# A two-layer decoder step on one core: a fifth raw weight tile in the place of a state tile, the samples' gathers moved to GpSimd, and score banks copied out twice instead of three times

## The chip, the cores and the metric

The kernel runs on one core of one Trainium2 chip. The metric is device microseconds (us) from the start to the end of one execution of the program. The engines that matter are the tensor engine (PE in the profile; PEld is its weight load), the vector engine (DVE), the scalar engine (ACT), GpSimd (POOL) and the sync engine (SP), whose queue issues nearly all DMAs here.

## What is computed

One inference step of a two-layer trunk: 272 prompt positions (16 learned ones and 256 given ones) and 8 samples of one position each share all weights, so that every product has 280 columns. Layer 0 is RWKV-7 time mixing with 64 heads of 64; layer 1 is sliding-window attention over one shared K and V. The change touches layer 0 alone:

```python
def rwkv7_step(S, inp):
    r, d, k, v, kk, b = inp
    sa = jnp.einsum('bhij,bhj->bhi', S, kk)
    S = S * d[:, :, None, :] - sa[..., None] * b[:, :, None, :] + v[..., None] * k[:, :, None, :]
    return S, jnp.einsum('bhij,bhj->bhi', S, r)

def rwkv7_layer(xn, shift_prev, S0, ...):
    rkvz = jnp.einsum('btpd,pde->btpe', xm[:, :, :4], w_rkvz)      # 4 products, 2048 x 4096 each
    ...                                                            # r, k, v, z, decay d, kk, b per head
    S_fin, y = lax.scan(rwkv7_step, S0, (r, d, k, v, kk, b))       # prompt: 272 steps; samples: 1 step each
    ...                                                            # group norm of y, bonus, gate silu(z)
    return y @ w_out, S_fin, xn[:, -1]
```

## The kernel before

**Products.** All weights come from memory as float32 tiles of 128 x 512 (256 KB, two blocks of 128 rows by 256 columns), named `raw_...` (line 200). ACT casts each to a high part `whi` (line 184), DVE subtracts to get the low part `wlo` (line 186), and PE multiplies three times per block: `whi` by the high and by the low part of the activations and `wlo` by the high part (lines 207 to 209). `raw` has four buffers, `whi` and `wlo` five each. In the stages after layer 0's middle part a second pool `rawx` of four takes every other tile.

**The long middle part** (`phase_a`, in the profile some 150 to 1350 us) runs these products and, between them, the recurrence of the prompt as matrix algebra on chunks of 64 positions. `drive` (line 590) writes the order of PE by hand. It counts positions, one per piece of a product (`products`, line 689: six matmuls of 128 x 128 by 280). Side streams are generators: what they yield is the number of positions until they are taken up again, or a condition. `main` (644) runs the chains of chunks (`chain`), the scores and the solving of triangular blocks; `preps` (662) prepares two heads' pairs at a time (`prep`, u = 0 to 15); `decodes` (681) does the samples; `late_gates` (1376) loads the gated activations for the output product once the last chain and the last group of samples are done. All other engines get an order from a scheduler that follows PE's positions and their dependences; each engine then works through its own queue in order, and so does SP.

**prep** (836) loads `kT`, `rT` and `vT` by DMA, computes `kk`, `a` (its tile is named `ta`) and the decay products `Pp`, and gathers the eight samples' columns of six tensors in one tile `sm`: six copies of 128 x 16 on ACT (line 910). PE transposes `sm` eight positions after `vT` was asked for (913).

**scores** (960) multiplies keys with queries in PSUM banks `ps_sc` (992) and empties each bank with ACT copies to `ND` (997, 998) and `N12` (999), beside two masked multiplications on DVE (1000, 1002). `substitute` (1033) takes `ND` on POOL (lines 1044 to 1047: `Noff`, `nd`, `N16`), then DVE inverts blocks of 16 in place and transposes them (`NL`, `TN`). `solve` (1069) waits a fixed number of positions and joins the blocks on PE (`ps_so`, 1082 to 1109) with copies by DVE and ACT between them (`ET`, `TT`, 1104 and 1112); `N12` is read at 1100.

**decode** (1246) goes through the samples' states, 16 heads at a time (g = 0 to 3), in eight slices of 256 KB: DMA to `dS` (1271), then two multiplications to `dT` and two sums on DVE (1275, 1276). `dS` has two buffers, and slices advance only while `self.samples` is true, that is while a chain runs. A slice is asked for right after the one before it was used, and used 8 positions later (5 for g = 3).

## Time and profile before

| | us |
|---|---|
| median of 3 runs | 2190.12 |
| lowest and highest of them | 2186.92, 2193.9 |
| the profiled execution, its own time | 2201.98 |
| span of its instructions | 2200.2 |

The profiled execution is 0.5% above the median. The profile names idle time of an engine with what ended it ("<- ACT cl L861" is a wait that ended when ACT had written `cl` at line 861). Numbers of buffers and layers in names are left out, so that `ps_so` stands for all banks of the solving. In the views of waits the three numbers are the us in total, the times, and the longest one. In the timeline a bracket gives the idle time before an instruction and what ended it. In the windows an engine's number is its busy time and the bracket the count of its instructions; PEclk is the share of TensorE's clock that was granted. A busy PE is not PE at its peak, since the ends of its matmuls are modelled.

### The profile page before, as it was taken

How to read it: one execution, taken by the hardware profiler on the slowest of the kernel's cores; microseconds unless marked ns; L12 is line 12 of the kernel's file. 1: busy time of each engine (PE TensorE's matmuls, PEld its weight loads, DVE VectorE, ACT ScalarE, POOL GpSimd, SP SyncE). 2: the span in 40 equal slices, each digit the busy share in tenths (PEclk: the TensorE clock that was granted, in tenths of full speed). 3: DMA queues.
4: the chain of work that ended last, by engine and by line, in shares of the span. 5: the costliest groups of instructions: out<-in, count | busy, mean ns of one | idle time of the engine just before them, and what ended most of it. 6: DMA issues, size and time to landing. Idle time of an engine off the chain costs nothing.

```text
span 2200.2 us, 56108 instructions
## 1 busy us (share of the span) xinstructions
PE 2122.6 (96%) x21556; PEld 2015.7 (92%) x21556; DVE 1716.4 (78%) x4115; ACT 1272.9 (58%) x2916; POOL 83.4 (4%) x100
## 2 busy tenths in 40 slices
PE   9999999999999998999999999999999999999997
PEld 7998899999889898888889899998999999999997
DVE  7956767787587776877887786997888888888885
ACT  3456756675666656756666454564565556555443
POOL 0010000000000000100001000110000000000000
PEclk9999999999999999999999999999999999999999
DMA  6997667757656776665645878766554544577774
GB/s 235 320 316 233 191 192 236 210 175 258 198 171 187 235 226 178 203 196 173 207 138 156 276 228 251 241 213 200 157 160 139 168 145 135 167 209 242 231 225 136
DMA packets 277444, 448.51 MB, mean 204 GB/s; under 512 B 53352, under 2 KB 99112, under 8 KB 276784
## 3 DMA queue, kind: packets, MB, share of 16 engines
q1 hardware_dynamic: 276888, 443.89, 65.1%
q8 instruction: 169, 2.77, 0.5%
q10 hardware_dynamic: 288, 1.05, 0.1%
q14 instruction: 99, 0.81, 0.1%
HBM read 382.81 MB, written 66.15 MB: 204 GB/s over the span
## 4 chain that ended last, share of the span: by engine, by line
PE 82%; DMA 6%; DVE 6%; ACT 4%; issue 2%; SPq 0%; DVEq 0%; POOLq 0%; ACTq 0%
PE ps_z L207 6%; PE ps_z L208 5%; PE ps_z L209 5%; PE ps_ob L209 3%; PE ps_ob L208 3%; PE ps_v L207 3%; PE ps_ob L207 3%; PE ps_q L209 3%; PE ps_q L207 3%; PE ps_q L208 3%; PE ps_k L207 3%; PE ps_v L208 3%; PE ps_v L209 3%; PE ps_k L209 2%; PE ps_k L208 2%; PE ps_r L207 2%
## 5 line engine op out<-in xcount | busy, mean ns | idle before, releaser
L207 PE MATMUL ps_z<-mhlm,whi_z 128*128 128x280 f32 x512 | 160.9, 314 | 1.1 <-ACT st L770 1.1
L208 PE MATMUL ps_z<-mhlm,whi_z 128*128 128x280 f32 x512 | 152.2, 297 | 2.1 <-issue 2.1
L207 PE MATMUL ps_q<-bmh,whi_qb 128*128 128x264 f32 x512 | 150.5, 294 | 2.4 <-ACT whi_qb L184 2.4
L209 PE MATMUL ps_z<-mhlm,wlo_z 128*128 128x280 f32 x512 | 152.0, 297 | 0.0
L209 PE MATMUL ps_q<-bmh,wlo_qb 128*128 128x264 f32 x512 | 146.7, 286 | 1.5 <-DVE wlo_qb L186 1.5
L207 PE MATMUL ps_z<-bmh,whi_zb 128*128 128x264 f32 x512 | 147.5, 288 | 0.0
L208 PE MATMUL ps_q<-bml,whi_qb 128*128 128x264 f32 x512 | 146.1, 285 | 0.0
L208 PE MATMUL ps_z<-bml,whi_zb 128*128 128x264 f32 x512 | 145.5, 284 | 0.0
L209 PE MATMUL ps_z<-bmh,wlo_zb 128*128 128x264 f32 x512 | 145.5, 284 | 0.0
L207 PE MATMUL ps_ob<-ghi,whi_ob 128*128 128x264 f32 x512 | 145.3, 285 | 0.0
L209 PE MATMUL ps_ob<-ghi,wlo_ob 128*128 128x264 f32 x512 | 144.9, 285 | 0.0
L208 PE MATMUL ps_ob<-glo,whi_ob 128*128 128x264 f32 x512 | 144.5, 283 | 0.0
L186 DVE TENSOR_TENSOR wlo_r<-raw_r,whi_r 128x512 fp32r<-128x512 f32 x128 | 87.8, 688 | 64.9 <-ACT whi_r L184 63.9
L184 ACT CAST whi_oa<-raw_oa 128x512 fp32r<-128x512 f32 x128 | 78.9, 620 | 101.2 <-DMA raw_oa<-a_w_out 31.7
L184 ACT CAST whi_ob<-raw_ob 128x512 fp32r<-128x512 f32 x128 | 79.2, 621 | 97.1 <-PE ps_ob L208 80.2
L186 DVE TENSOR_TENSOR wlo_v<-raw_v,whi_v 128x512 fp32r<-128x512 f32 x128 | 87.9, 691 | 53.0 <-ACT whi_v L184 48.7
L207 PE MATMUL ps_k<-mhlm,whi_k 128*128 128x280 f32 x384 | 121.9, 317 | 1.9 <-ACT whi_k L184 1.6
L207 PE MATMUL ps_v<-mhlm,whi_v 128*128 128x280 f32 x384 | 121.4, 316 | 1.9 <-ACT st L770 1.9
L186 DVE TENSOR_TENSOR wlo_z<-raw_z,whi_z 128x512 fp32r<-128x512 f32 x128 | 88.6, 695 | 35.7 <-ACT whi_z L184 32.7
L186 DVE TENSOR_TENSOR wlo_oa<-raw_oa,whi_oa 128x512 fp32r<-128x512 f32 x128 | 87.5, 689 | 35.4 <-ACT whi_oa L184 31.7
L186 DVE TENSOR_TENSOR wlo_k<-raw_k,whi_k 128x512 fp32r<-128x512 f32 x112 | 76.0, 687 | 49.5 <-ACT whi_k L184 49.1
L184 ACT CAST whi_zb<-raw_zb 128x512 fp32r<-128x512 f32 x128 | 78.3, 619 | 62.5 <-PE ps_z L208 42.0
(462 smaller groups left out, 7739.5 us busy)
## 6 DMA issues: line engine op xcount, KB each, us to landing
raw_k<-a_w_rkvz SPq DMA_DIRECT2D x128, 256.0 KB
raw_v<-a_w_rkvz SPq DMA_DIRECT2D x128, 256.0 KB
raw_r<-a_w_rkvz SPq DMA_DIRECT2D x128, 256.0 KB
raw_z<-a_w_rkvz SPq DMA_DIRECT2D x128, 256.0 KB
raw_oa<-a_w_out SPq DMA_DIRECT2D x128, 256.0 KB
raw_qb<-b_w_qz SPq DMA_DIRECT2D x128, 256.0 KB
raw_zb<-b_w_qz SPq DMA_DIRECT2D x128, 256.0 KB
raw_ob<-b_w_o SPq DMA_DIRECT2D x128, 256.0 KB
```

The costliest lines, as they stand in the source:

```text
L184: self.nc.scalar.copy(hi, src)
L186: return self.nc.vector.tensor_tensor(lo, src, hi.bitcast(F32), op=ALU.subtract)
L207: mm(ps, wh, xh, start=start, stop=False)
L208: mm(ps, wh, xl, start=False, stop=False)
L209: return mm(ps, wl, xh, start=False, stop=stop)
```

## The change

Four edits:

- `raw` gets five buffers instead of four, `dS` one instead of two. A slice of the samples' state is now asked for 3 positions after the one before it was used, and used 5 positions later (4 for g = 3).
- The six gathering copies of `prep` go from ACT to POOL (16 preps, so 96 copies).
- `ND` and `N12` become two halves of one tile `F`. For the upper 32 rows of a half bank one ACT copy of 64 columns takes the place of two of 32: 64 copies fewer. `F` is one tile for the whole kernel, where `N12` was taken anew for each chain.
- By the yields the streams stand at other positions.

```diff
             else:
-                raw = t("raw", F32, bufs=4)
+                raw = t("raw", F32, bufs=5)
...
-        self.ND = t([128, 20, 32], "ND")
+        self.F = t([128, 20, 64], "F")
+        self.ND, self.N12 = self.F[:, :, 0:32], self.F[:, 0:16, 32:64]
...
         for i, x in enumerate((kk, a, kT, rT, vT, Pp[:, :, 5:])):
-            A.copy(sm[:, :, i], x[:, :, L:N])
+            G.tensor_copy(sm[:, :, i], x[:, :, L:N])
...
-        if u % 2 == 0:
-            self.N12 = rp.tile([128, 16, 32], F32, tag="N12", name=f"N12_{u}")
-        N12 = self.N12
...
-                A.copy(inst(self.ND, r1, cs), pv[r1, :, :, 0:32])
+                A.copy(inst(self.F, r1, cs), pv[r1, :, :, 0:64])
                 A.copy(inst(self.ND, r2, cs), pv[r2, :, :, 32:64])
-                A.copy(inst(N12, r1, cs), pv[r1, :, :, 32:64])
...
         for q in range(64 // NI):
-            S = rp.tile([128, NI, 64], F32, tag="dS", bufs=2, name=f"dS{g}_{q}")
+            if q:
+                yield 3
+            S = rp.tile([128, NI, 64], F32, tag="dS", bufs=1, name=f"dS{g}_{q}")
             T = rp.tile([128, NI, 64], F32, tag="dT", bufs=1, name=f"dT{g}_{q}")
             ...
-            yield 8 if g < 3 else 5, lambda: self.samples
+            yield 5 if g < 3 else 4, lambda: self.samples
```

The first place where the order differs is POOL's queue at the fourth substitution (the tile `sm` belongs to the prep of u = 8, the four other rows to the substitution). Before:

```order
L1047 TENSOR_TENSOR Noff<-ND,consts 128x16x16
L1044 TENSOR_TENSOR nd_9508<-ND,consts 128x320
L1045 TENSOR_TENSOR nd_9509<-ND,consts 128x320
L1046 TENSOR_TENSOR N_1734<-nd_9508,nd_9509 128x320
L1133 MEMSET X_4_11387 64x256 x2
```

After:

```order
L911 COPY sm_10058<-rT_9632 128x2x8
L1044 TENSOR_TENSOR Noff<-F,consts 128x16x16
L911 COPY sm_10058<-kk_9634 128x2x8
L911 COPY sm_10058<-Pp 128x2x8
L1041 TENSOR_TENSOR nd_9546<-F,consts 128x320
L1042 TENSOR_TENSOR nd_9547<-F,consts 128x320
L1043 TENSOR_TENSOR N_1734<-nd_9546,nd_9547 128x320
```

Three gathers now stand ahead of `nd` in POOL's queue.

The second place is SP's queue at the last group of samples (`dS3`), between the raw tiles of the first output product. Before:

```order
L1271 DMA dS3_3_19278<-state_wkv 128x1x512
L200 DMA raw_oa1_512_6_19397<-a_w_out 128x512
L200 DMA raw_oa1_512_8_19466<-a_w_out 128x512
L1271 DMA dS3_4_19363<-state_wkv 128x1x512
L200 DMA raw_oa1_512_10_19507<-a_w_out 128x512
L200 DMA raw_oa1_512_12_19545<-a_w_out 128x512
L1271 DMA dS3_5_19457<-state_wkv 128x1x512
```

After:

```order
L1270 DMA dS3_4_19558<-state_wkv 128x1x512
L781 DMA xd_159<-xr1_4_19223 128x2x280
L200 DMA raw_oa1_1024_2_19719<-a_w_out 128x512
L718 DMA xr1_8_19759<-xT 128x2x280
L200 DMA raw_oa1_1024_4_19761<-a_w_out 128x512
L1270 DMA dS3_5_19669<-state_wkv 128x1x512
```

The slices stand two product groups later (column 1024 instead of 512), and the transposition `ps_dy` of the last group stands 27 positions later on PE, while the last chain (`ps_wu` of chain 7) stands 13 positions later; the end of the first output product stays where it was.

The third place is SP's queue where `late_gates` loads `gy` and `gz` (560 or 544 KB each). Before:

```order
L1360 DMA gy4_20068<-yd4_216 128x1120
L1360 DMA gy5_20105<-yd5_217 128x1120
L200 DMA raw_oa1_1280_0_20118<-a_w_out 128x512
L200 DMA raw_oa1_1280_2_20149<-a_w_out 128x512
L1358 DMA gz6_20137<-zd6_194 128x1120
L717 DMA xr1_10_20172<-xT 128x2x280
L200 DMA raw_oa1_1280_4_20174<-a_w_out 128x512
L1358 DMA gz7_20344<-zd7_195 128x1120
```

After:

```order
L1359 DMA gy4_20261<-yd4_216 128x1120
L1359 DMA gy5_20298<-yd5_217 128x1120
L1357 DMA gz6_20341<-zd6_194 128x1120
L1357 DMA gz7_20396<-zd7_195 128x1120
L200 DMA raw_oa1_1536_14_20365<-a_w_out 128x512
```

The four loads stand later, and no raw tile stands between them.

More of the change, by code (lines that the diff above doesn't have):

```diff
@@ L573, in phase_a @@
         ms = nc.gpsimd.memset
-        for a in (self.KB, self.ND, self.N16, self.Noff, self.Y):
+        for a in (self.KB, self.F, self.N16, self.Noff, self.Y):
             ms(a, 0.0)
```

## The prediction

> **What bounds the kernel now.** I read the page first, then busy time by stretches, then who PE and ACT wait for, then the timeline at the waits.

> ```profile
> PE 2122.6 (96%) x21556; PEld 2015.7 (92%) x21556; DVE 1716.4 (78%) x4115; ACT 1272.9 (58%) x2916; POOL 83.4 (4%) x100
> PE 82%; DMA 6%; DVE 6%; ACT 4%; issue 2%; SPq 0%; DVEq 0%; POOLq 0%; ACTq 0%
> 1350.00:1400.00 50.00, 50.00 (x389) 50.00 (x388) 38.17 (x62) 24.33 (x44) 5.42 (x6) 1.00 0.74 224
> 150.00:1300.00 1150.00, 1096.83 (x13429) 1024.11 (x13428) 875.35 (x1948) 735.50 (x1745) 45.10 (x47) 0.98 0.66 202
> 1300.00:1500.00 200.00, 194.94 (x1488) 191.95 (x1487) 167.79 (x311) 104.00 (x187) 16.84 (x18) 1.00 0.77 238
> 1500.00:1900.00 400.00, 396.17 (x3361) 381.13 (x3360) 323.83 (x1188) 228.53 (x620) 1.10 (x2) 1.00 0.51 157
> ```

> PE is the bound: 2122.6 of 2200.2 us, and 82% of the chain. No edit takes work from PE, so the change can only win PE's idle time and clock. In the stretch 150 to 1300, where three of the edits act, PE is idle for 1150 - 1096.83 = 53.2 us, and it was granted 0.98 of its clock, which is some 23 us more. From 1300 to 1900 only 5.1 + 3.8 us are idle. A change that won all of it would stop at some 80 us; what can be won is that part of it which ends on ACT or on a raw tile.

> ```profile
> PE ps_l L207 <- ACT cl L861: 5.5, 6, 2.0
> PE ps_so L1109 <- ACT ET L1104: 4.6, 3, 1.9
> PE ps_q L207 <- ACT whi_qb L184: 2.4, 1, 2.4
> PE ps_k L207 <- ACT whi_k L184: 1.6, 1, 1.6
> PE ps_sm L913 <- ACT sm L910: 1.6, 2, 1.2
> ACT sm L910 <- DMA rT<-rd: 24.7, 15, 4.2
> ACT sm L910 <- DMA vT<-vd: 15.2, 8, 4.3
> ACT whi_k L184 <- DMA raw_k<-a_w_rkvz: 22.0, 12, 7.1
> ACT whi_r L184 <- DMA raw_r<-a_w_rkvz: 20.8, 12, 3.6
> ```

> PE's waits are small and scattered, and ACT ends most of the ones above. ACT itself stands 24.7 + 15.2 = 39.9 us at the gathering copies, waiting for a tile of which it wants eight columns. Everything queued behind on ACT stands with it.

> **The gathers leave ACT.** Two places show what such a wait costs PE:

> ```profile
> 828.76 0.20 ACT L910 COPY sm<-rT 128x16 f32<-128x16 f32 x1 [4.25 <-DMA rT<-rd]
> 829.29 0.74 ACT L1183 COPY X<-ps_wu 64x256 f32<-64x256 f32 x2
> 829.70 1.07 PE L1184 MATMUL ps_sy<-X,BK 128*64 128x64 f32 x16 [1.60 <-ACT X L1183]
> 966.81 0.21 ACT L910 COPY sm<-rT 128x16 f32<-128x16 f32 x1 [2.17 <-DMA rT<-rd]
> 967.04 0.58 ACT L1104 COPY ET<-ps_so 32x512 f32<-32x512 f32 x1
> 967.67 1.82 PE L1109 MATMUL ps_so<-TT,ET 32*32 32x32 f32 x64 [1.91 <-ACT ET L1104]
> 829.50:835.00 5.50, 5.24 (x48) 4.97 (x49) 4.04 (x9) 2.21 (x6) 0.00 (x0) 0.69 1.03 296
> 967.50:975.00 7.50, 7.33 (x106) 7.00 (x108) 3.22 (x6) 3.80 (x10) 0.00 (x0) 0.54 0.60 160
> ```

> ACT stood 4.25 us for `rT`, the copy of `X` came late, and PE stood 1.60 us; the second time it was 1.91 us behind `ET`. Right after both, PE ran on a reduced clock: (1 - 0.69) x 5.5 = 1.7 us and (1 - 0.54) x 7.5 = 3.45 us of work lost. With the 1.6 us in which PE waited for `sm` itself this is 1.60 + 1.91 + 5.15 + 1.6 = 10.3 us. POOL, busy for 4% of the span, waits instead, and PE reads `sm` only eight positions after `vT` was asked for. Bounds: 5.2 us if the clock drops anyway and POOL brings `sm` no sooner (1.60 + 1.91 + 1.7); 13 if one more clock drop goes (another 3.45). I take 10.3.

> [...]

> **Less work on ACT.**

> ```profile
> 150.00:1300.00 1150.00, 19.36 (x96) 0.98 0.66 202
> 150.00:1300.00 1150.00, 16.36 (x64) 0.98 0.66 202
> 822.36 0.37 ACT L1173 COPY W<-ps_wu 128x256 f32<-128x256 f32 x1
> L997 ACT COPY ND<-ps_sc x64: 252/256/259, 191.8 to 1190.3; 32x128 f32<-32x128 f32 x64
> ```

> The 96 gathers take 19.36 us and the 64 copies to `N12` 16.36. The copy that does the work of two writes 256 elements per row; the nearest row of that size takes 0.37 us, against 0.256 for the old one: 64 x 0.114 = 7.3 us come back. ACT loses 19.4 + 16.4 - 7.3 = 28.5 of 735.5 us, 4%, and a burst of six copies shrinks by 0.3 us. What is left of the waits quoted first, 5.5 for `cl` and 4.6 - 1.9 for `ET`, is 8.2 us. Bounds 0 and 8.2; I take the middle, 4.

> **The fifth raw tile.** PE spends 50 us on 389 matmuls of 280 columns, 0.129 us each, and a tile feeds 12 of them, so that SP may ask 1.55 us earlier. ACT's waits for raw tiles (22.0 and 20.8 above) hardly reach PE, since `whi` and `wlo` have five buffers. PE's own waits that a raw tile can end are 2.4 (`whi_qb`) and 1.6 (`whi_k`). Where `rawx` alternates with `raw`, its four buffers still set how far SP gets, and nothing changes. Bounds 0 and 4; I take 3.

> **One state buffer.** The load is now asked for 5 positions ahead, 4 in the last group, where it was 8 and 5.

> ```profile
> 1252.74 0.63 SPq L1271 DMA_DIRECT2D dS<-state_wkv  x1
> 1258.55 0.68 DVE L1275 TENSOR_TENSOR dT<-dS,ve 128x512 f32<-128x512 f32 x1
> 171.33 3.56 DMA raw_r<-a_w_rkvz
> 1317.19 5.96 DMA raw_oa<-a_w_out
> 821.79 9.13 DMA raw_v<-a_w_rkvz
> ```

> Five positions were 1258.55 - 1252.74 = 5.8 us; four are then 4.65. Loads of the same size landed after 3.56 to 9.13 us. If one is late, DVE stands at `dT`, and behind it `wlo`, the chain's state `FS` and the solving's copies. ACT's 39.9 us at the gathers cost PE 10.3, a share of 0.26. At 5.96 us the 28 loads that follow another slice wait 7 x 1.3 + 21 x 0.15 = 12.3 us, which costs PE 3.2; at 9.13 they wait 7 x 4.5 + 21 x 3.3 = 101 us, which costs 26; at 3.56 nothing. I take 3, since the chain of waits holds more loads near 5.9 than near 9.

> **The gates' loads come later and together.**

> ```profile
> 1300.00:1350.00 50.00, 48.24 (x364) 46.69 (x363) 36.38 (x71) 23.05 (x36) 0.00 (x0) 1.00 0.93 302
> gz<-zd SPq DMA_DIRECT2D x2, 560.0 KB
> ```

> Four such loads, 4 x 573 KB at the 302 GB/s of that window, are 7.6 us in which no raw tile moves. The tile behind them is wanted nine tiles later (five raw, four split), 14 us ahead, so most is covered; it costs 0 to 7.6, and I take 2. The 27 positions by which the last group ends later cost nothing by themselves: the first output product still stands after it.

> **POOL as a neighbour of DVE.**

> ```profile
> L1047 POOL TENSOR_TENSOR Noff<-ND,consts x8: 731/1096/2558, 229.2 to 1191.0; 128x256 f32<-128x256 f32 x8
> L277 POOL TENSOR_SCALAR par<-par x1: 286/286/286, 10.9 to 10.9; 128x32 f32<-128x32 f32 x1
> 1061.73 1.11 DVE L882 TENSOR_TENSOR kT<-kT,km 128x280 f32<-128x280 f32 x1
> L882 DVE TENSOR_TENSOR kT<-kT,km x32: 405/440/1125, 166.1 to 1134.4; 128x280 f32<-128x280 f32 x32
> ```

> The same instructions take 0.73 to 2.56 us on POOL and 0.44 to 1.1 on DVE: they get in each other's way. A gather on POOL should take no more than the 0.286 of twice its size. If each held DVE for all of it, 96 x 0.286 = 27 us of DVE at the share of 0.26 would cost 7 us; nearly all DVE rows stand at their median, so 1. [...]

> **Sum:** -10.3 - 4 - 3 + 3 + 2 + 1 = -11.3 us, from the profiled 2202.0 to 2190.7. That execution is 0.54% above the median, so the median goes from 2190.1 to 2179. What a measurement of this kernel can tell from no change is 0.3%, 6.6 us.

> **Rivals.**
> - *The waits only move.* Streams stand 8 to 13 positions later, so each copy meets another neighbour; PE's 53.2 us are scattered over many small rows, and the two large ones came from chance meetings. Then -10.3 becomes about -4, and the sum -5 with the rest: 2185. Against it: the 39.9 us leave ACT wherever they fall.
> - *The clock drops stay.* They may come from all idle time of their neighbourhood and not from the one stall; then 5.15 of the 10.3 go, and -6.2 is left: 2184. The two windows speak against it. [...]
> - *POOL holds DVE* for the whole of each gather: 7 instead of 1, -5.3: 2185. The medians of DVE's rows speak against it, the 1.11 us for it. [...]
> - *DVE takes ACT's place (slower).* Loads of the state land as `raw_v` at 821.79 did. Then +26 stands for +3: +11.7, 2202. It decides once DVE waits over 14.3 / 0.26 / 28 = 2 us per slice. Against it: five positions sufficed in the last group before.
> - *POOL delays the substitution (slower).* Gathers of `kk` and `Pp` stand ahead of `nd`. If each of the eight substitutions came later by the longest row's excess, 2.56 - 0.73 = 1.8 us, and lost 1.7 us of clock: 8 x 3.5 = 28 against -11: 2207. For it, the order; against it, POOL's idleness.
> - *ACT's relief goes further.* If the 8.2 us and half of the 23 us of clock went, where I count 4 and 5.15: -22, 2168.

> **How the numbers follow.** Forecast 0.48 (its own range 2171 to 2188), moved waits 0.17, clock 0.06, POOL holding DVE 0.05, DVE 0.10, late substitution 0.04, more relief 0.10. Faster by over 0.3%, below 2183.5: 0.40 of the forecast, 0.07 of the three small ones, all 0.10: 0.57. Slower, above 2196.7: the two slower rivals with 0.14 and 0.03 of the moved waits: 0.17. Within: the rest, 0.26. The range goes from 2158, a little past the larger relief, to 2202, the DVE case.

> **What would show it.** Right: ACT has no row of waits for `rT` or `vT` at the gathers, POOL has them; PE's idle time in 150 to 1300 falls from 53 to some 42 us and its clock rises; the copies of 64 columns to `F` take 0.37 us. Wrong: DVE has rows that wait for `dS`, `ps_so` waits for `TN`, PE waits for `sm` from POOL, or PE stands around 1340 behind raw tiles. The forecast falls if the clock stays at 0.98 though the two stalls are gone.

## The result and the profile after

| | before | after |
|---|---|---|
| median of the runs, us | 2191.13 (2186.92 to 2193.9, 4 runs) | 2159.05 (2156.8 to 2160.89, 4 runs) |
| ratio, 95% interval | | 0.9855 [0.9835, 0.9875] |
| the profiled execution, us | 2201.98 | 2157.39 |
| span, us | 2200.2 | 2155.6 |

The change saved 1.45%, 32 us in these runs. Two later measurements of the same two kernels gave 0.9884 and 0.9890, so some 24 to 32 us. The forecast was -11.3 us. One execution each of e13 and e15 below fell out, with 9290 and 7466 us, and their medians and ratios leave it out.

The busy times on the page of the changed kernel:

```profile
PE 2102.4 (98%) x21556; PEld 2001.5 (93%) x21556; DVE 1709.1 (79%) x4115; ACT 1260.4 (58%) x2756; POOL 136.4 (6%) x196
```

Its busy time by stretches, the three that were shown of before (length, then PE, PEld, DVE, ACT, POOL with their counts, PE's clock, DMA share, GB/s):

```profile
150.00:1300.00 1150.00, 1118.57 (x13756) 1050.65 (x13755) 895.64 (x2003) 738.62 (x1612) 97.50 (x143) 0.99 0.69 212
1300.00:1500.00 200.00, 193.27 (x1473) 190.25 (x1472) 168.54 (x342) 109.34 (x223) 17.89 (x20) 0.98 0.74 226
1500.00:1900.00 400.00, 399.78 (x3413) 386.15 (x3413) 336.07 (x1172) 230.58 (x596) 0.00 (x0) 1.00 0.52 156
```

PE's idle time from 150 to 1300 us fell from 53.2 to 31.4 us and its clock rose from 0.98 to 0.99. From 1500 to 1900 us 3.8 us of idle time became 0.2. From 1300 to 1500 us the changed kernel is worse: 6.7 us idle against 5.1, and a clock of 0.98 against 1.00. The two profiles overstate the gain: their spans differ by 44.6 us, since the profiled execution of before was 0.5% above its median. Who waits now, from the view of waits (us in total, times, longest):

```profile
PE ps_so L1079 <- DVE TN L1058: 6.5, 2, 4.0
PE ps_wu L1163 <- ACT X L1197: 3.5, 4, 2.3
ACT whi_v L184 <- DMA raw_v<-a_w_rkvz: 12.3, 8, 2.6
ACT whi_r L184 <- DMA raw_r<-a_w_rkvz: 6.0, 4, 2.0
ACT whi_k L184 <- DMA raw_k<-a_w_rkvz: 5.9, 5, 1.8
ACT whi_z L184 <- DMA raw_z<-a_w_rkvz: 2.9, 2, 2.4
DVE dT L1274 <- DMA dS<-state_wkv: 21.3, 12, 3.8
POOL sm L911 <- DMA rT<-rd: 210.0, 14, 29.4
```

And the group of the copies to `F` (times in ns, shortest, median, longest):

```profile
L995 ACT COPY F<-ps_sc x64: 361/363/366, 185.1 to 1159.5; 32x256 f32<-32x256 f32 x64
```

ACT has no row for the gathers any more, and POOL stands for `rT` instead. ACT's waits for `raw_k` and `raw_r`, 22.0 and 20.8 us before, are 5.9 and 6.0. DVE has 21.3 us of new waits for `dS`. The copies to `F` take the 0.37 us that were forecast.

### The profile page after: what moved, and what is told of

Its sections match the earlier page's. It is cut to its first block, busy times and chain, and to the rows that moved or that the text cites. A ratio compares the mean times of both kernels' runs of the same rounds, so it can differ in the third digit from the quotient of the medians.

```text
span 2155.6 us, 56147 instructions
## 1 busy us (share of the span) xinstructions
PE 2102.4 (98%) x21556; PEld 2001.5 (93%) x21556; DVE 1709.1 (79%) x4115; ACT 1260.4 (58%) x2756; POOL 136.4 (6%) x196
## 4 chain that ended last, share of the span: by engine, by line
PE 59%; DVE 4%; DMA 2%; ACT 2%; issue 2%; SPq 0%; DVEq 0%; POOLq 0%; ACTq 0%
PE ps_z L207 5%; PE ps_z L208 5%; PE ps_z L209 5%; PE ps_ob L209 3%; PE ps_ob L208 3%; PE ps_ob L207 3%; PE ps_q L207 3%; PE ps_q L209 3%; PE ps_q L208 3%; PE ps_oa L208 2%; PE ps_oa L207 2%; PE ps_oa L209 2%; PE ps_o L207 1%; PE ps_o L209 1%; PE ps_o L208 1%
## 5 line engine op out<-in xcount | busy, mean ns | idle before, releaser
L207 PE MATMUL ps_z<-mhlm,whi_z 128*128 128x280 f32 x512 | 158.2, 309 | 1.1 <-ACT st L771 1.1
L207 PE MATMUL ps_q<-bmh,whi_qb 128*128 128x264 f32 x512 | 149.9, 293 | 0.1
L208 PE MATMUL ps_z<-mhlm,whi_z 128*128 128x280 f32 x512 | 149.6, 292 | 0.0
L207 PE MATMUL ps_z<-bmh,whi_zb 128*128 128x264 f32 x512 | 147.5, 288 | 0.0
L207 PE MATMUL ps_ob<-ghi,whi_ob 128*128 128x264 f32 x512 | 145.2, 284 | 0.0
L184 ACT CAST whi_ob<-raw_ob 128x512 fp32r<-128x512 f32 x128 | 79.2, 621 | 97.0 <-PE ps_ob L208 80.3
L184 ACT CAST whi_oa<-raw_oa 128x512 fp32r<-128x512 f32 x128 | 79.0, 620 | 89.7 <-PE ps_oa L208 27.1
L207 PE MATMUL ps_v<-mhlm,whi_v 128*128 128x280 f32 x384 | 120.7, 314 | 0.0
L207 PE MATMUL ps_k<-mhlm,whi_k 128*128 128x280 f32 x384 | 120.1, 313 | 0.0
L184 ACT CAST whi_v<-raw_v 128x512 fp32r<-128x512 f32 x128 | 78.7, 618 | 64.0 <-PE ps_v L208 35.0
L184 ACT CAST whi_zb<-raw_zb 128x512 fp32r<-128x512 f32 x128 | 78.3, 620 | 62.5 <-PE ps_z L208 38.5
```

The source lines that it names most:

```text
L184: self.nc.scalar.copy(hi, src)
L207: mm(ps, wh, xh, start=start, stop=False)
L208: mm(ps, wh, xl, start=False, stop=False)
```

## Experiments

The kernels ran in batches, each on one chip with its own runs of the kernel before, whose median (given in the first row of each batch) differs a little. Numbers are compared within a batch or by their ratio to before; 0.001 is 2.2 us. The batches of e5 and of e9 ran on the same chip. A difference of two ratios is uncertain by some 4 to 6 us.

| run | what it is | median us | before | ratio [95%] |
|---|---|---|---|---|
| e1 | before + gathers on GpSimd | 2182.09 | 2189.52 | 0.9967 [0.9953, 0.9981] |
| e2 | before + two copies | 2183.41 | | 0.9981 [0.9962, 1.0001] |
| e3 | before + five raw, one state, new yields | 2169.86 | | 0.9915 [0.9894, 0.9937] |
| e4 | before + new yields | 2176.88 | | 0.9948 [0.9929, 0.9966] |
| e5 | changed, four raw | 2180.44 | 2184.15 | 0.9974 [0.9958, 0.9989] |
| e6 | changed, gathers on ACT | 2162.13 | | 0.9894 [0.9873, 0.9915] |
| e7 | changed, 96 more ACT copies | 2160.66 | | 0.9888 [0.9868, 0.9908] |
| e8 | changed, last group sooner | 2166.48 | | 0.9909 [0.9886, 0.9931] |
| e9 | changed | 2158.96 | 2185.81 | 0.9884 [0.9865, 0.9904] |
| e10 | before + new yields, first three groups | 2174.91 | | 0.9955 [0.9938, 0.9972] |
| e11 | before, loads asked for one position later | 2189.87 | | 1.0017 [0.9998, 1.0037] |
| e12 | before, slices seven positions apart | 2186.68 | | 1.0005 [0.9991, 1.0019] |
| e13 | changed, old positions | 2180.24 | 2188.90 | 0.9964 [0.9950, 0.9978] |
| e14 | changed, four raw, two states | 2168.46 | | 0.9916 [0.9895, 0.9937] |
| e15 | before + gathers and copies | 2173.56 | | 0.9935 [0.9917, 0.9954] |
| e16 | changed, loads one position sooner | 2154.29 | | 0.9852 [0.9833, 0.9870] |
| e17 | e16 again | 2156.46 | 2186.47 | 0.9867 [0.9840, 0.9893] |
| e18 | changed | 2160.09 | | 0.9890 [0.9866, 0.9915] |

### One part alone: e1 to e4

e1 has the line `G.tensor_copy(sm[:, :, i], ...)` alone, e2 the tile `F` with its two copies alone, e4 the yields alone, e3 the yields with the two numbers of buffers:

```diff
# e3 and e4
+            if q:
+                yield 3
-            yield 8 if g < 3 else 5, lambda: self.samples
+            yield 5 if g < 3 else 4, lambda: self.samples
# e3 alone
-                raw = t("raw", F32, bufs=4)
+                raw = t("raw", F32, bufs=5)
-            S = rp.tile([128, NI, 64], F32, tag="dS", bufs=2, name=f"dS{g}_{q}")
+            S = rp.tile([128, NI, 64], F32, tag="dS", bufs=1, name=f"dS{g}_{q}")
```

> The kernel before with the 96 gathers on GpSimd and nothing else changed. Waits (the 39.9 us that ACT stood at the gathers cost PE far more than the two stalls I counted): some 20 us faster, PE idle in 150 to 1300 down from 53 to about 38, half the low-clock stretches gone. Load (only the 19.4 us of work count): about 9 us faster. Positions or raw tile: within 4 us of before.

> The kernel before with the score banks copied out twice and nothing else changed; ACT loses 64 x 0.256 us and gets 64 x 0.11 back, 9.5 us. Load: about 6 us faster, a third of what both ACT edits give. Waits: 0 to 4 us faster. Positions or raw tile: no change.

> The kernel before with five raw tiles, one state tile and the new yields; both ACT edits left out. Raw tile: 15 us faster or more, ACT's waits for raw tiles halved. Waits or load: between 4 us faster and 4 us slower, with some 20 us of DVE waits for the state slices, which was 3 us for and 3 us against in the prediction.

> The kernel before with the new yields alone: four raw tiles, two state tiles, so that only the positions of the streams move. Positions (the stalls were chance meetings that other positions miss): 10 us faster or more. All other theories: within 5 us of before.

Measured, by the ratios: gathers -7.2 us, copies -4.2 (its interval just reaches no change), yields -11.4, yields with the exchange of tiles -18.6. The parts that the prediction put at nothing in all gave more than the two it counted on.

In e1 one of the prediction's two stalls is gone, and PE's waits for `ET` fell from 4.6 to 1.7 us. The other one moved. Where ACT had stood 4.25 us for `rT`, the timeline of e1 has:

```profile
823.88 0.62 ACT L184 CAST whi_v<-raw_v 128x512 fp32r<-128x512 f32 x1 [4.64 <-DMA raw_v<-a_w_rkvz]
827.51 0.40 PE L207 MATMUL ps_l<-lt4h,lhi 96*128 96x280 f32 x1 [2.02 <-DVE ks L815]
```

DVE stands with ACT, PE stands 2.02 us behind DVE's `ks` instead of 1.60 behind ACT's `X`, and 3.41 us at half clock follow as before. It is the same in sum: over k, r, v and z ACT's waits for raw tiles were 64.8 us before and are 87.8 in e1 (87.6 in e15). More than half of the 39.9 us that left ACT at the gathers came back at the casts behind them. PE's waits for `sm` stayed too, at 1.4 us, now for POOL.

### Which positions: e10, e11, e12

What the yields do on PE was not in the prediction's three places. The first slice of a group is used 5 positions after its load was asked for and not 8; therefore the last slice of group 0 still falls into a chain, where before it had to wait for the next chain, and `ps_dy0` stands 86 positions sooner. It pushes the scores behind it on by 8 positions, and from there the solving and the chains stand 8, later 13 positions later against the products.

```diff
# e10 against before
+            if q:
+                yield 3 if g < 3 else 0
-            yield 8 if g < 3 else 5, lambda: self.samples
+            yield 5 if g < 3 else 5, lambda: self.samples
# e11 against before
+            if q:
+                yield 1 if g < 3 else 1
-            yield 8 if g < 3 else 5, lambda: self.samples
+            yield 7 if g < 3 else 6, lambda: self.samples
# e12 against before
-            yield 8 if g < 3 else 5, lambda: self.samples
+            yield 7 if g < 3 else 5, lambda: self.samples
```

> The kernel before with the new yields for the first three groups of samples alone; the last group keeps the old ones. On PE the transposition of group 0 (ps_dy0) stands 86 positions sooner, because its last slice is still taken within a chain, and from there on scores, solving and chains stand 8, later 13 positions later. Theory Shift (the 11 us of the yields alone come from the other positions): 2172 to 2180 beside 2189, so 9 to 17 us faster than before. Theory Tail (they come from the last group's end): within 4 us of before.

> The kernel before with each slice asked for one position after the one before it was used, and used seven positions later: the loads are asked for one position later, and PE's order stays as before, but for the last three groups' transpositions (1 to 14 positions). Theory Asks (the queue of loads gains when a slice doesn't come straight after the one before it was used): 5 us and more faster than before. Theory Shift: within 4 us of before.

> The kernel before with slices seven positions apart for the first three groups (eight before), asked for at once as before. Group 0 again ends sooner (ps_dy0 by 90 positions), and the streams behind it stand 7 positions later. Theory Shift in its form 'the old positions were unlucky': 5 to 15 us faster than before. In its form 'the new positions are lucky': within 5 us of before, either way.

e10 has the gain of e4 (0.9955 against 0.9948), so nothing shows of the last group's new yields by themselves. Its end is not back in its old place, though: in e10 it still stands some 20 positions later than before (27 in e4), since the groups ahead of it moved. e11, which moves loads and hardly anything on PE, gains nothing; neither does e12, which shifts the same streams by 7 positions all the way. So it is not "any shift" that gains, but this one. From 720 to 1265 us, busy time of the kernel before:

```profile
720.00:1265.00 545.00, 511.45 (x6380) 476.44 (x6379) 424.93 (x955) 341.10 (x797) 27.50 (x24) 0.97 0.65 200
```

and its waits there:

```profile
PE ps_wu L1181 <- ACT W L1173: 1.6, 2, 1.4
PE ps_so L1109 <- ACT ET L1104: 1.9, 1, 1.9
ACT sm L910 <- DMA rT<-rd: 12.8, 6, 4.2
```

Busy time of e10 in the same stretch:

```profile
720.00:1265.00 545.00, 524.64 (x6623) 489.99 (x6623) 439.35 (x985) 351.00 (x815) 23.10 (x22) 0.99 0.67 207
```

and its waits:

```profile
PE ps_so L1082 <- DVE TN L1061: 5.5, 1, 5.5
PE ps_wu L1181 <- ACT W L1173: 0.7, 1, 0.7
ACT sm L910 <- DMA rT<-rd: 7.1, 6, 1.9
```

Busy time of e12:

```profile
720.00:1265.00 545.00, 514.37 (x6450) 479.59 (x6449) 431.45 (x964) 342.60 (x801) 25.10 (x22) 0.98 0.66 203
```

and its waits:

```profile
PE ps_wu L1181 <- ACT W L1176: 3.1, 1, 3.1
PE ps_o L207 <- ACT st L770: 3.3, 1, 3.3
ACT sm L910 <- DMA rT<-rd: 10.2, 5, 2.9
```

At the new positions PE stands 20 us in these 545 instead of 34, and ACT's waits at the gathers shrink without a gather being moved. They brought one large wait of their own, 5.5 us behind `TN`, where the kernel before has no wait for `TN` above 1.3 us in this stretch. At seven positions PE stands 31 us, behind other copies. Which of the meetings makes the difference was not settled.

### The exchange of tiles: e5 and e14

```diff
# e5 and e14 against the changed kernel
-                raw = t("raw", F32, bufs=5)
+                raw = t("raw", F32, bufs=4)
# e14 alone
-            S = rp.tile([128, NI, 64], F32, tag="dS", bufs=1, name=f"dS{g}_{q}")
+            S = rp.tile([128, NI, 64], F32, tag="dS", bufs=2, name=f"dS{g}_{q}")
```

> The changed kernel with four raw tiles (one state tile and the new yields stay). Theory Raw (the fifth tile is worth the difference of the two runs before, 2176.9 - 2169.9, some 7 us): 5 to 9 us slower than the changed kernel, that is 2164 to 2168. Theory Positions (all of that edit is the yields): within 3 us of the changed kernel, 2156 to 2162.

> The changed kernel with four raw tiles and two state tiles, PE's order as in the changed kernel. Beside e5 (four raw, one state, 2180.4) it prices the second state tile, beside the changed kernel the exchange of the two. Theory State (one state tile costs, DVE stands for dS 16 to 21 us): 5 us and more below e5, 2168 to 2175, and DVE's rows for dS are gone. Theory Covered (it costs nothing): within 3 us of e5.

Without the fifth tile the changed kernel loses 20 us (0.9974 against 0.9884 on the same chip), three times what the theory had. The second state tile gives 12.7 back (0.9974 to 0.9916, on another chip). Both together, the exchange is worth 7.0 us here (e14 to the changed kernel) and 7.2 between e4 and e3; the split into 19.7 and 12.7 holds for this order of the steps. Waits of ACT and PE in e5:

```profile
ACT whi_k L184 <- DMA raw_k<-a_w_rkvz: 21.7, 14, 7.2
ACT whi_v L184 <- DMA raw_v<-a_w_rkvz: 19.0, 16, 3.4
ACT whi_r L184 <- DMA raw_r<-a_w_rkvz: 16.3, 15, 3.5
ACT whi_z L184 <- DMA raw_z<-a_w_rkvz: 12.9, 13, 2.2
PE ps_wu L1178 <- ACT W L1170: 3.1, 3, 1.5
PE ps_q L207 <- ACT whi_qb L184: 2.4, 1, 2.4
```

Its busy time where the products `ps_q` begin:

```profile
1500.00:1525.00 25.00, 21.50 (x159) 20.17 (x155) 18.82 (x67) 13.38 (x34) 0.00 (x0) 0.93 0.70 211
```

ACT stands 69.9 us for these four names; with the fifth tile it was 27.1. Only the row of `ps_q` names a raw tile's cast; that place costs 3.5 us of idle time and 0.07 x 25 = 1.75 us of clock, and both are gone in the changed kernel. The larger part is not under a raw tile's name. The timeline of e5 shows how it gets to PE:

```profile
424.23 0.62 ACT L184 CAST whi_v<-raw_v 128x512 fp32r<-128x512 f32 x1 [3.25 <-DMA raw_v<-a_w_rkvz]
425.24 0.62 ACT L184 CAST whi_v<-raw_v 128x512 fp32r<-128x512 f32 x1 [0.39 <-PE ps_v L209]
425.88 0.37 ACT L1170 COPY W<-ps_wu 128x256 f32<-128x256 f32 x1
426.31 0.51 PE L1178 MATMUL ps_wu<-W,TT 64*64 64x64 f32 x10 [1.08 <-ACT W L1170]
```

ACT stood 3.25 us for `raw_v`, the casts ran one behind the other, `W` came after them, and PE stood 1.08 us for `W`. It is the same path by which a gather's wait reached PE.

Over the whole span PE is idle for 65 us in e5 and for 51 to 53 in three profiles of the changed kernel. Of that, 22.0 us end on ACT in e5 and 13.6 to 15.4 in those three, 22.4 and 15.6 to 18.8 on DVE, and the stretches at half clock cost 18.8 us against 10.2 to 13.7. So the fifth tile's gain is spread over many waits; one of them is shown above, and they were not counted one by one. ACT's waits for raw tiles alone do not give the time either: e14 has 85.0 us of them, more than e5, and is faster.

### Waits or work on ACT: e6, e7, e15

e6 puts `A.copy` back in the changed kernel's gathers. e15 is the kernel before with the gathers on GpSimd and `F`. e7 adds, beside each gather:

```diff
             G.tensor_copy(sm[:, :, i], x[:, :, L:N])
+            two = self.par2[:, 0:16].rearrange("p (a b) -> p a b", a=2)
+            A.copy(two, two)
```

> The changed kernel with the gathers back on ScalarE, PE's order the same. Theory Waits (ACT stands for rT and vT, and PE behind ACT): 5 to 12 us slower than the changed kernel, and rows ACT sm <- DMA rT are back with some 40 us. Theory Positions (such waits hurt only where the old positions let them meet PE): within 3 us of it, with those rows back all the same.

> The changed kernel with six more ACT copies of 128x16 in each prep, which wait for no load (they copy a table onto itself, 96 copies, some 19 us of ACT work); the gathers stay on GpSimd. Theory Load (what counted was ACT's work): as slow as the run with the gathers back on ScalarE, 5 us and more above the changed kernel. Theory Waits: within 3 us of the changed kernel.

> The kernel before with the gathers on GpSimd and two copies, raw tiles, state tiles and positions as before. Theory Sum: the two gains alone (0.33% and 0.19%) add up, ratio 0.993 to 0.996, some 9 to 14 us. Theory Overlap (both free the same stalls of ScalarE): no more than the larger of them, ratio 0.996 to 0.998.

The two edits on ACT give 14.2 us together (0.9935). But in the changed kernel the gathers can go back to ACT for 2 to 3 us, which is inside the noise, though ACT then stands as long as it did before, by the waits of e6:

```profile
ACT sm L911 <- DMA rT<-rd: 24.3, 14, 5.5
ACT sm L911 <- DMA vT<-vd: 16.7, 8, 5.3
```

So some 40 us of waiting were worth 7 us alone and 2 to 3 with the other edits in place; the two values are no further apart than their noise. e7's added work costs 1 to 2 us, inside the noise too.

### The state's room: e8, e13, e16 to e18

```diff
# e8 and e13 against the changed kernel
-                yield 3
+                yield 3 if g < 3 else 1
# e13 alone
-            yield 5 if g < 3 else 4, lambda: self.samples
+            yield (5 if q else 8) if g < 3 else (4 if q else 5), lambda: self.samples
# e16 and e17 against the changed kernel
-                yield 3
+                yield 2
-            yield 5 if g < 3 else 4, lambda: self.samples
+            yield (6 if q else 5) if g < 3 else (5 if q else 4), lambda: self.samples
```

> The changed kernel with one position instead of three between the slices of the last group of samples, so that this group ends with the last chain (13 instead of 27 positions later than before). Theory Tail (the 8.7 us given back between 1300 and 1380 us of the profile are the price of side work put there): 3 to 7 us faster than the changed kernel, 2152 to 2156. Theory Covered (that stretch only takes the side work that the middle part lost): within 2 us of it.

> The changed kernel with the first slice of each of the first three groups used 8 positions after its load was asked for, and the last group's slices 5 apart: PE's order is again that of the kernel before, with all other edits in place (five raw tiles, one state tile, gathers on GpSimd, two copies; loads of the state asked for 3, in the last group 1 position after the slice before was used). Theory Sum (each part is worth what it was worth alone): 9 to 15 us slower than the changed kernel's 2159.0, that is 2168 to 2174. Theory Overlap (the new positions and the edits on ScalarE and raw tiles remove the same stalls): within 5 us of the changed kernel.

> The changed kernel with each further slice asked for 2 positions after the one before it was used instead of 3, and used 6 (last group 5) positions later instead of 5 (4); PE's order stays that of the changed kernel. Theory State (DVE's 21 us of waits for dS cost PE some 5): the rows of DVE for dS fall below 10 us and the time by 2 to 6 us, to 2153 to 2157. Theory Queue (asked for sooner, the load stands in SP's queue until DVE has left the one tile, and raw tiles stand behind it): 3 us and more slower.

> The kernel of e16 again, now on one chip with the changed kernel, since e16's waits for dS had not fallen (20.9 against 21.3 us) though its time was 2154.3. If asking one position sooner gains by itself, it is 3 to 6 us below the changed kernel on this chip; if e16's chip was the difference, within 2 us of it.

> The changed kernel itself once more, beside the kernel before, so that the runs before can be set against it: ratio 0.985 to 0.989. If it is near 0.985, the four raw tiles of e5 cost some 26 us and ACT's extra work in e7 some 7; if it is near 0.989, they cost some 19 us and nothing.

> The changed kernel on the same chip as e17: 2157 to 2161, 3 to 6 us above e17 if asking sooner gains, within 2 us of it if the chips differed.

e8 came out on neither theory's side: 7.5 us above the 2158.96 of the changed kernel on the same chip, 5.5 by the ratios, whose intervals overlap. DVE's waits for the state in e8:

```profile
DVE dT L1274 <- DMA dS<-state_wkv: 33.2, 15, 3.8
```

Its busy time where the last group and the last chain run:

```profile
1200.00:1345.00 145.00, 134.27 (x1489) 128.17 (x1488) 104.92 (x212) 62.95 (x117) 1.61 (x2) 0.96 0.70 219
```

Two places of its timeline:

```profile
1232.86 0.69 DVE L1274 TENSOR_TENSOR dT<-dS,ve 128x512 f32<-128x512 f32 x1 [2.85 <-DMA dS<-state_wkv]
1233.59 0.29 DVE L1197 COPY X<-FS 64x256 f32<-64x256 f32 x1
1233.93 0.87 PE L1163 MATMUL ps_wu<-X,E 128*64 128x64 f32 x12 [3.09 <-DVE X L1197]
...
1246.79 0.69 DVE L1274 TENSOR_TENSOR dT<-dS,ve 128x512 f32<-128x512 f32 x1 [2.49 <-DMA dS<-state_wkv]
1248.33 0.44 DVE L766 TENSOR_TENSOR xr<-ps_o,xr 128x280 f32<-128x280 f32 x1
1248.82 0.60 PE L207 MATMUL ps_o<-mhlm,whi_oa 128*128 128x280 f32 x1 [3.63 <-DVE xr L766]
```

With one state tile and slices five positions apart, DVE stands 2.85 us for `dS`, the chain's `X` comes late, and PE stands 3.09 us, then 3.63 for `xr`. The changed kernel leaves seven positions per slice in the last group. Its busy time in that stretch, with PE idle for 3.7 us and not 10.7, and more clock:

```profile
1200.00:1345.00 145.00, 141.26 (x1438) 135.81 (x1437) 111.59 (x224) 67.81 (x126) 3.21 (x4) 0.98 0.74 228
```

e13 has PE's order of before with all other edits, and is 17 us slower than the changed kernel by the ratios (0.9964 against 0.9884), and 6 slower than e15, which lacks the exchange and ran beside it. Some 5 to 8 of the 17 are the last group's five positions, if these cost what they cost in e8.

e16 and e17 ask one position sooner. They measured 2154.3 and, beside the changed kernel's 2160.1, 2156.5. Both beat the kernel before (0.9852, 0.9867). Against the changed kernel the 3.6 us of the last batch point the same way, but the intervals overlap (0.9840 to 0.9893 and 0.9866 to 0.9915). The expected cause did not show: DVE's waits for `dS` were 20.9 us in e16 and 23.3 in e17, against 21.3.

## Why the prediction came out 13 to 21 us short

The sum of the runs, each step by ratios: both edits on ACT -14.2 (e15), new positions on top of them -4.2 (e14), one state tile +12.7 (e5), fifth raw tile -19.7 (changed), together -25, each step uncertain by 4 to 6 us. The prediction had -14.3, 0, +3, -3, and +3 for side effects. Taken as one, the exchange of tiles gave 7 us where the prediction had nothing. The side effects are inside the steps.

**Gathers and less work on ACT: right in sum, in part by luck.** -10.3 - 4 against -14.2 (10 to 18 by its interval); alone they gave 7.2 and 4.2. Of the two stalls the second went as forecast; the first came back under other names, in e1 behind `raw_v` and in the changed kernel behind `dS`. The 1.6 us for `sm` did not go: PE waited for it from POOL for 1.4 us in e1 and for 1.1 to 3.1 in three profiles of the changed kernel. And the prediction's word against *The waits only move*, that the 39.9 us leave ACT wherever they fall, was wrong: 23 us of them came back at raw tiles. The 7.2 lies between that rival's 4 and the forecast's 10.3. The lower bound of 5.2 was also summed wrong: it stands for the case that the clock drops anyway, and still counts one of the two drops; without it, it is 3.5.

**The fifth raw tile: the step that failed most.** "ACT's waits for raw tiles hardly reach PE, since `whi` and `wlo` have five buffers", bounds 0 and 4. It is true of the products, and it only asked for PE's rows that name `whi`. But ACT works in order, so that a late raw tile holds up `W` (in e5 3.25 us for `raw_v`, and behind it 1.08 us of PE for `W`) just as a late `rT` holds up `X`, which the prediction itself had shown two paragraphs earlier. ACT's waits for raw tiles (64.8 us over k, r, v and z before) were larger than the 39.9 at the gathers; at the share of 0.26 that it used elsewhere, the 42.8 us that the fifth tile took from them (69.9 - 27.1) would have made 11, where e5 shows 19.7. And the bound of 2.4 for `whi_qb` left out the clock behind it (1.75).

**One state buffer: too small, and its path shown only in part.** It counted 12.3 us of waits of DVE and 3 us of PE. DVE waited 16.3 us in e5 and 15.8 to 21.3 in three profiles of the changed kernel, and the price was 12.7: 0.78 for each of e5's 16.3 us, where the prediction took over the 0.26 that it had worked out for ACT. That a late slice holds PE through DVE and the chain's `X` is seen in e8, and in the changed kernel near the place of the prediction's first stall:

```profile
821.61 0.69 DVE L1274 TENSOR_TENSOR dT<-dS,ve 128x512 f32<-128x512 f32 x1 [3.84 <-DMA dS<-state_wkv]
822.80 0.41 ACT L1197 COPY X<-FS 64x256 f32<-64x256 f32 x1 [5.75 <-DVE FS L1194]
823.26 0.33 PE L1163 MATMUL ps_wu<-X,E 128*64 128x64 f32 x2 [2.30 <-ACT X L1197]
```

DVE stands 3.84 us, PE 2.30 us in the end, and 3.41 us at half clock follow. A wait for DVE's `X` (5.5 us at line 1166) was one of PE's three largest rows already before, and the prediction's list leaves it out. The names of PE's waits do not show the whole price: those that end on DVE are 22.4 us in e5 and 25.4 in e14, which has two state tiles, and those that end on ACT 22.0 and 17.7. So how most of the 12.7 us reach PE stays open. SP's queue is another candidate: in e5 SP itself stood 4.7 us at these loads, with raw tiles behind them, and in e14 not at all. The rival *DVE takes ACT's place* was half true: DVE stood, and the fifth raw tile more than paid for it.

**Positions: the step that was missing.** The prediction followed only the last group's 27 positions. It gave no term to the 8 to 13 positions by which nearly all other streams moved, though its own rival said that the two large stalls came from chance meetings. Chance meetings can go as well as move: the new positions gave 11 us alone (e4), 4 on top of the edits on ACT (e14 against e15), and 10 to 12 with all edits in place (e13, less what e8 cost). With 4 to 6 us of noise on each, how far they and the edits on ACT remove the same stalls is not shown.

**Side effects: the gates cost more than their +2, and by another path.** The changed kernel around 1300 us:

```profile
1299.14 1.53 DVE L1364 SCALAR_TENSOR_TENSOR gy<-gz,gy 128x280 f32<-128x280 f32 x4 [2.56 <-issue]
1300.70 1.12 ACT L184 CAST ghi<-gy 128x1120 fp32r<-128x1120 f32 x1 [5.56 <-DVE gy L1364]
1302.40 0.40 PE L207 MATMUL ps_o<-mhlm,whi_oa 128*128 128x280 f32 x1 [1.99 <-ACT whi_oa L184]
1302.80:1309.63 6.83, 5.91 (x26) 5.79 (x26) 5.57 (x11) 3.02 (x6) 0.00 (x0) 0.50 1.01 356
```

The prediction looked for a raw tile that comes late behind the four loads. What happens is that ACT stands 5.56 us for the multiplied gate `gy`, the cast of `whi_oa` stands behind it, PE waits 1.99 us, and the 6.83 us behind that run at half clock, which is 3.4 us more. PE's waits for `whi_oa` here are 2.0 to 3.7 us in every profile whose last group ends later than before, e8 excepted, and 0.7 at most in the others. So the 27 positions did cost something, against "cost nothing by themselves"; e8 gets rid of this stall and pays for it earlier, around 1240 us. What DVE waited for at 1299 us the profile does not name. Nothing of the +1 for POOL as a neighbour was told apart, but the gathers took 58.3 us on POOL and not the 27 that were allowed.

*POOL delays the substitution* did not come: DVE's waits for `N` from POOL went from 2.9 to 5.5 us in all, and they are 6.3 in e4, where no gather is on POOL. Its sign, `ps_so` behind `TN`, did appear, with 6.5 us after. Before it had 1.7 us. The row of e4:

```profile
PE ps_so L1082 <- DVE TN L1061: 7.0, 2, 5.2
```

With the gathers on POOL at the old positions (e15) it is 3.1 us. So most of it came with the positions.

**The clock.** It rose as forecast: from 150 to 1300 us there are 12 stretches at half clock before, 10 in e1 and 4 after. *The clock drops stay* did not come: 4 are left of 12. Drops came behind stalls as short as the two of the forecast, 1.60 and 1.91 us: of the 162 stretches at half clock in all twenty profiles up to 2100 us, 147 came without a stall of 3.41 us, the length of the shortest stretch, right before them, and 66 behind one of 1 to 2 us at the longest. The rival's premise, that all idle time of the neighbourhood counts, is close to what the last section finds.

**The low end.** *ACT's relief goes further* named the time nearest to the measured one, 2168, but not the cause: ACT's two edits gave 14.2 us and not 22. That the range reached down to 2158 on its account is luck.

## What to carry to other kernels

Count an in-order engine's waits by what stands behind them, whatever their names: a row such as "ACT whi <- raw" belongs in the sum when copies of the critical chain share that queue. A share that turns one engine's waits into the bound's idle time was not the same from one engine and one version of this kernel to the next (by the ratios 0.18 for the 39.9 us at the gathers in e1, 0.46 for the 42.8 us at the raw tiles and 0.78 for the 16.3 us at the state, both from e5), so work it out anew for each. Waits that leave one place in a queue can come back at the next, as 23 of those 39.9 us did: ask what the engine will stand for instead. Where an edit shifts side streams against the main one, price the shift by a run with the shift alone, and do not take for granted that gains add.

## What the runs showed of the hardware

```profile
753.26:756.67 3.41, 0.75 (x5) 0.51 (x5) 3.41 (x8) 1.37 (x6) 2.06 (x1) 1.00 0.28 79
756.67:760.08 3.41, 3.41 (x22) 3.15 (x22) 2.06 (x7) 2.03 (x5) 2.73 (x5) 0.50 0.31 83
760.08:763.50 3.42, 3.42 (x38) 3.20 (x35) 2.98 (x9) 3.03 (x7) 0.00 (x0) 1.00 0.27 77
```

PE was busy 0.75 of 3.41 us, and the next slot ran at half clock. Over the slots from 150 to 2100 us of all twenty profiles, worked out from PE's records: behind a slot in which PE was busy less than 40% the next one was at half clock in 75 of 75 cases, at 40 to 50% in 38 of 45, at 50 to 60% in 35 of 85, at 60 to 70% in 21 of 122, and above 90% in 15 of 10,609. A slot at half clock costs 1.7 us (0.50 x 3.41). By these counts a stall's price would depend on whether it falls within one slot or is split by two: two stalls of 1 us each in one slot could cost more than one of 2 us across a border. That is an estimate from the counts and was not tried.

A gather of 128x16 on POOL took 0.19 us at the shortest, 0.61 in the mean and 4.04 at the longest in the changed kernel, where the forecast allowed 0.286. The 13 of the 96 that ran beside no DVE instruction took 0.191 to 0.199 us; of the 83 others 46 took more than 0.25. In the profile of before, 27 of DVE's 32 multiplications to `kT` (L882) ran beside no POOL instruction and took 0.405 to 0.451 us; the five others took 0.435 to 1.125.
